# Scratch places given out by a planner's clock instead of a count of instructions, with the planner's durations booked anew

## The chip, the cores and the metric

The kernel runs on one core of one Trainium2 chip. The metric is device time in microseconds (us) from the first to the last instruction of one execution, with what lies around it; the time before is the median of three runs. Shorter is better.

## The reference, cut to what matters

One inference step of a one-layer hybrid decoder, all in float32, for a prompt of 272 positions (16 learned meta tokens and 256 tokens) and for 8 sequences of 4 new tokens: 304 columns in all, each 2048 long.

```
xn = rms_norm(x, norm_mix);  z = xn @ w_in             # 2048 -> 7456 columns
z_a, z_b = z[..., :RWKV_COLS], z[..., RWKV_COLS:]
o_a, S_a = rwkv7_mixer(z_a, shifted z_a, S_a0, ...)    # 16 heads of 64, a recurrence over positions
o_b, S_b = retention_mixer(z_b, S_b0, ...)             # 4 heads of 256, in chunks
h = x + concat([o_a, o_b]) @ w_out
hn = rms_norm(h, norm_ffn)
h = h + (silu(hn @ w_gate) * (hn @ w_up)) @ w_down     # 2048 -> 5632 -> 2048
y = rms_norm(h, norm_final)                            # and the new states
```

The weights are read once, 512 KB at a time. They and the activations are split into a high and a low part (`hi` and `lo`, of a type that TensorE takes in one pass), so a weight tile of 128 by 128 costs three matmuls: high by high, high by low, low by high.

## The kernel before

**Two kinds of work.** `main` (L609) walks through the weights in a fixed sequence: the input projection (59 column tiles), the output projection, then gate, up and down of the feed-forward part. For each step it loads (`wr`, four buffers), casts on ScalarE (`wh`), subtracts on VectorE (`wl`, the two with four buffers each) and issues three matmuls into an accumulator `acc`. Beside it run *streams*: Python generators that do the mixing of the finished columns. There is one for each of 8 pairs of RWKV heads (`pair` with `inverse`, `units`, `sample`, `pair_out`), one for each of 4 retention heads (`ret`), and small ones that empty an accumulator (`evacuate`, `mixed`) or bring a pair's small weights (`lora_weights`). Their matmuls go to `mm`. All streams belong to the first part of the run, in which TensorE has the input projection to do between them.

**What sets the order.** The kernel builds itself twice. In a first pass, the draft, a `Plan` books every instruction on a clock of its own for each engine: `book` (L346) works out when the operands are ready and adds a duration from a small table; `array` does so for TensorE. `pick` (L422) is asked before every step of `main`: the first stream whose booked time of readiness has passed goes on to its next `yield`, else `main` takes a step. The choices go into a log, and the second pass, which writes the real program, replays it. Every engine then runs its own instructions strictly in that order, and an instruction that waits holds up all behind it on its engine. Loads and stores are all issued by SyncE (SP), also in order.

**Where scratch lives.** Tiles of the streams come from `Step.t` (L550). In the draft each gets a tensor of its own. `Room.place` (L470) then gives each a place in one of two long tiles, the arenas (`arena_dt.float` for F32 and `arena_dt.float32r` for F32R in the profile, 33000 columns together), so that tiles whose lives don't overlap may share columns. A life here runs from the tile's creation (`note`) to its last use (`use`), both counted in instructions booked so far by all engines, plus a slack of 40, 20, 10, 5 or 0 instructions, whichever first fits; among five orders of packing the smallest is taken. The count says which instruction comes first in the program. It doesn't say which comes first in time, since engines run apart by microseconds. So the layer that writes the program must make the first writer of a place wait, with semaphores, until the last reader of the tile that had it before is done. The draft doesn't know these waits, since its tiles share nothing.

Helpers record every instruction, so that all have one line in the profile (L300); tiles tell them apart. Names used below: `lora` is the DRAM tensor of the pairs' small weights (two loads for each pair, by `lora_weights`), `s0w` the RWKV states (one for each pair), `s0r` the retention states (four for each retention head) and `rmask` its masks (one for each head). In `inverse`, five `stream_shuffle` instructions fill a tile `rs` three times for each pair, GpSimd multiplies from it, and VectorE then writes the masked tiles `em`.

Of the kernel before, what the change touches and what calls it, by code (L numbers as in the profile page):

```python
# [9 lines left out]
F32R = mybir.dt.float32r  # L10
# [65 lines left out]
KEYS = ((0, META, SEQ, 0), (P, P, NP - P, SEQ), (LASTK, 2 * P, T - 2 * P, SEQ + NP - P))  # L76
RMW = SEQ + NP - P + T - 2 * P
ROOM = 33000


def zcols():
# [53 lines left out]
def constants():  # L135
# [169 lines left out]
class Plan:  # L305
# [5 lines left out]
    def __init__(self, nc, rooms, draft, log, keep):  # L311
        self.keep = keep
        self.rooms, self.draft, self.log, self.count = rooms, draft, log, 0
        self.clock = dict(PE=0.0, DVE=0.0, ACT=0.0, POOL=0.0, SP=0.0)
        self.end = self.dma = 0.0
        self.uses, self.outside = {}, ()
# [29 lines left out]
    def book(self, eng, what, a, k):  # L346
        self.count += 1
        if not self.draft:
            return
        aps = [x for x in (*a, *k.values()) if hasattr(x, "shape")]  # L350
        for x in aps:
            for room in self.rooms.values():
                room.use(x, self.count)
        out, ins = aps[0], aps[1:]

        at = 0.0
        boxes = [(x.name, self.box(x), x is out) for x in aps if x.name not in self.outside]
        meet = lambda a, b: a[0] < b[1] and b[0] < a[1] and a[2] < b[3] and b[2] < a[3]
        for name, box, writes in boxes:
            for other, done, by, written in self.uses.get(name, ()):  # L360
                if (written or writes) and done + 100 > at and not (by == eng == "PE") and meet(box, other):
                    at = max(at, done + (30 if by == eng else 100 if eng == "PE" else 60))
        n = math.prod(out.shape[1:])
        if eng == "PE":
            done = self.array(what, *a[:3], at) + 170
        elif eng == "SP":
            self.clock[eng] = at = max(self.clock[eng] + 400, at)
            self.dma = max(self.dma, at + 1400) + 4 * out.shape[0] * n / 320
            done = self.dma + 600
# [84 lines left out]
class Room:  # L454

    def __init__(self):
        self.spans, self.index, self.places, self.size, self.taken = [], {}, None, 0, 0

    def note(self, ap, size, count):
        self.index[ap.name] = len(self.spans)
        self.spans.append([size, count, count])

    def use(self, x, count):
        i = self.index.get(getattr(x, "name", None))
        if i is not None:
            self.spans[i][2] = count

    def place(self, limit):  # L470


        for slack in (40, 20, 10, 5, 0):
            best = None
            for key in (lambda n, a, b: (-n, a), lambda n, a, b: (-n * (b - a), a), lambda n, a, b: (a - b, -n),
                        lambda n, a, b: (a, -n), lambda n, a, b: (-n // 256, a - b)):
                size, places = self.pack(key, slack)
                if best is None or size < best[0]:
                    best = size, places
            if best[0] <= limit:  # L480
                break
        self.size, self.places = best
        assert self.size <= limit, self.size

    def pack(self, key, slack):
        done, places = [], [0] * len(self.spans)
        for i in sorted(range(len(self.spans)), key=lambda i: key(*self.spans[i])):
            size, a, b = self.spans[i]
            size = -(-size // 8) * 8
# [6 lines left out]
            places[i] = at  # L496
            done.append((at, size, a, b))
        return max(o + n for o, n, _, _ in done), places

    def take(self, size):  # L500

# [14 lines left out]
class Step:  # L516
# [33 lines left out]
    def t(self, shape, tag, dt=F32, bufs=None, pool=None):  # L550
        self.n += 1
        if pool is not None:
            name = f"{tag}_{self.n}"
            old = self.tags.setdefault(tag, [])
            old.append(name)
            n = {"mm": 8 - ACC, "acc": ACC}.get(tag, bufs)
            if n and len(old) > n:
                self.plan.follows(name, old[-1 - n])
            return pool.tile(shape, dt, tag=tag, name=name, **({} if bufs is None else {"bufs": bufs}))
        size = math.prod(shape[1:])  # L560
        if self.draft:
            ap = self.mp.tile(shape, dt, tag=f"t{self.n}", name=f"{tag}_{self.n}")
            self.rooms[dt].note(ap, size, self.plan.count)
# [1148 lines left out]
def body(tc, I, O):  # L1712
    from contextlib import ExitStack
    gam4 = constants()[3]
    rooms = {F32: Room(), F32R: Room()}
    nc = draft(I, O)
    log = []
    Step(tile.TileContext(nc[0]).__enter__(), nc[1], nc[2], ExitStack(), rooms, True, log).build(gam4)
    rooms[F32R].place(4200)
# [25 lines left out]
```

## Time and profile before

| what | us |
|---|---|
| median of 3 runs (lowest, highest) | 1593.91 (1592.52, 1594.58) |
| the profiled execution's own time | 1595.29 |
| its span, first to last instruction | 1593.5 |
| TensorE (PE) busy | 1547.0, 97% |
| VectorE (DVE) busy | 1101.9, 69% |
| ScalarE (ACT) busy | 822.2, 52% |
| GpSimd (POOL) busy | 166.5, 10% |
| DMA, mean over the span | 158 GB/s, 252.49 MB |

The granted clock of TensorE is 0.996 of full speed over the run. Up to about 600 us the input projection and all mixing run side by side; after that only the output projection and the feed-forward part are left, and GpSimd has no work there. An entry `x <- y` in a list of waits is idle time of engine x that ended when y was done, and a bracket at the end of a row of the timeline gives the idle time just before that row. "issue" means that nothing was waited for that the profile shows.

### The profile page before, as it was taken

To read this page: it belongs to the slowest core of one execution; us is meant where nothing else is said; L and a number is where in the kernel's file an instruction comes from. 1 tells how busy PE (TensorE), PEld (TensorE's weight loads), DVE (VectorE), ACT (ScalarE), POOL (GpSimd) and SP (SyncE) were. 2 spreads that over 40 slices of the span, in tenths; PEclk is the share of its full clock that TensorE was granted. 3 is DMA by queue.
4 is the path that set the end of the run, shared out by engine and by line. 5 is a ranking of instruction groups with operands and counts; after the bars stand their busy time and mean duration, and the time that the engine had idled before them with its cause. 6 is when DMAs were issued, how large, how long until landed. Compare 5 with 4: busy or idle time off the path is not lost.

```text
span 1593.5 us, 30795 instructions
## 1 busy us (share of the span) xinstructions
PE 1547.0 (97%) x11388; PEld 1506.5 (95%) x11388; DVE 1101.9 (69%) x2590; ACT 822.2 (52%) x1795; POOL 166.5 (10%) x567
## 2 busy tenths in 40 slices
PE   9999999999999999999999999999999999999997
PEld 8888999898888899999999999999999999999997
DVE  7888888897879867777565656565655656565657
ACT  6657676747656564455444444444444444444445
POOL 0343414323041300000000000000000000000000
PEclk9999999999999999999999999999999999999998
DMA  7443343334543448655555555555555555555553
GB/s 263 144 123 112 114 126 113 101 113 133 157 156 117 143 149 278 231 163 157 169 164 165 168 170 159 169 166 168 166 166 172 160 165 167 172 162 170 162 168 116
DMA packets 76998, 252.49 MB, mean 158 GB/s; under 512 B 9392, under 2 KB 14640, under 8 KB 76848
## 3 DMA queue, kind: packets, MB, share of 16 engines
q1 hardware_dynamic: 76848, 250.52, 50.8%
q8 instruction: 90, 1.47, 0.4%
q14 instruction: 60, 0.49, 0.1%
HBM read 236.21 MB, written 14.28 MB: 157 GB/s over the span
## 4 chain that ended last, share of the span: by engine, by line
PE 71%; DVE 6%; DMA 2%; ACT 1%; issue 1%; POOL 1%; DVEq 0%; POOLq 0%; ACTq 0%; SPq 0%
PE acc L300 66%; PE mm L300 5%; DVE arena_dt.float L300 5%; DVE wl L300 1%; ACT arena_dt.float L300 1%; DMA arena_dt.float<-s0r 1%; POOL arena_dt.float L300 1%; DMA arena_dt.float<-lora 1%; DVE arena_dt.float32r L300 0%; ACT wh L300 0%; DVE xl L300 0%; ACT arena_dt.float32r L300 0%; DVEq L1741 0%; POOL shout L300 0%; POOLq L300 0%
## 5 line engine op out<-in xcount | busy, mean ns | idle before, releaser
L300 PE MATMUL acc<-xh,wh 128*128 128x288 f32 (+2 forms) x2592 | 791.7, 305 | 0.6 <-ACT wh L300 0.6
L300 PE MATMUL acc<-xh,wl 128*128 128x288 f32 (+2 forms) x2592 | 772.8, 298 | 13.3 <-DVE wl L300 13.2
L300 PE MATMUL acc<-xl,wh 128*128 128x288 f32 (+2 forms) x2592 | 766.8, 296 | 0.0
L300 ACT CAST wh<-wr 128x512 fp32r<-128x512 f32 x826 | 500.9, 617 | 363.8 <-PE acc L300 327.7
L300 DVE TENSOR_TENSOR wl<-wr,wh 128x512 fp32r<-128x512 f32 x826 | 562.8, 689 | 127.8 <-ACT wh L300 124.8
L300 PEld LDWEIGHTS acc<-xh,wl 128*128 128x128 f32 x2592 | 486.1, 188 | 19.7 <-DVE wl L300 18.9
L300 PEld LDWEIGHTS acc<-xh,wh 128*128 128x128 f32 x2592 | 487.8, 188 | 5.9 <-issue 1.3
L300 PEld LDWEIGHTS acc<-xl,wh 128*128 128x128 f32 x2592 | 486.9, 188 | 3.7 <-issue 0.5
L300 PE MATMUL acc<-arena_dt.float32r,wh 128*128 128x288 f32 x1408 | 280.0, 294 | 0.4 <-ACT arena_dt.float32r L300 0.3
L300 PEld LDWEIGHTS acc<-arena_dt.float32r,wh 128*128 128x128 f32 x1408 | 226.3, 188 | 0.9 <-ACT arena_dt.float32r L300 0.6
L300 PE MATMUL acc<-arena_dt.float32r,wl 128*128 128x288 f32 x704 | 208.0, 295 | 0.0
L300 DVE TENSOR_TENSOR arena_dt.float<-acc,arena_dt.float 128x288 f32<-128x288 f32 (+4 forms) x181 | 72.8, 420 | 167.1 <-PE acc L300 166.2
L300 PE MATMUL mm<-arena_dt.float 128*128 128x128 f32 (+6 forms) x1072 | 172.0, 311 | 15.4 <-ACT arena_dt.float L300 5.9
L300 PEld LDWEIGHTS mm<-arena_dt.float 128*128 128x128 f32 (+1 forms) x1072 | 138.1, 181 | 32.7 <-ACT arena_dt.float L300 8.5
L300 DVE TENSOR_TENSOR arena_dt.float<-arena_dt.float 128x288 f32<-128x288 f32 (+10 forms) x483 | 158.5, 355 | 10.8 <-ACT arena_dt.float L300 4.3
L300 DVE TENSOR_TENSOR arena_dt.float<-arena_dt.float,acc 128x288 f32<-128x288 f32 x208 | 94.4, 454 | 100.4 <-PE acc L300 99.9
L300 ACT ACTIVATE arena_dt.float<-arena_dt.float 128x288 f32<-128x288 f32 (+6 forms) x200 | 85.2, 433 | 122.7 <-DVE arena_dt.float L300 115.5
L300 ACT COPY arena_dt.float<-mm 64x64 f32<-64x64 f32 (+11 forms) x330 | 91.7, 286 | 80.6 <-PE mm L300 74.9
L300 PEld LDWEIGHTS acc<-arena_dt.float32r,wl 128*128 128x128 f32 x704 | 132.4, 188 | 0.0
L300 ACT CAST arena_dt.float32r<-arena_dt.float 128x288 fp32r<-128x288 f32 (+4 forms) x73 | 30.4, 423 | 124.2 <-DVE arena_dt.float L300 92.6
L300 POOL TENSOR_TENSOR arena_dt.float<-arena_dt.float 128x75 f32<-128x75 f32 (+14 forms) x240 | 86.9, 362 | 73.1 <-DVE arena_dt.float L300 50.1
L300 POOL MEMSET arena_dt.float<- 128x64 f32 (+8 forms) x137 | 29.7, 238 | 181.3 <-DVE arena_dt.float L300 102.9
(64 smaller groups left out, 675.5 us busy)
## 6 DMA issues: line engine op xcount, KB each, us to landing
wr<-big SPq DMA_DIRECT2D x409, 512.0 KB, 3.6
arena_dt.float<-s0r SPq DMA_DIRECT2D x16, 512.0 KB, 5.1
out_rts<-arena_dt.float SPq DMA_DIRECT2D x16, 512.0 KB, 5.6
arena_dt.float<-xT SPq DMA_DIRECT2D x4, 576.0 KB, 5.8
out_y<-arena_dt.float SPq DMA_DIRECT2D x8, 288.0 KB, 2.2
arena_dt.float<-xT SPq DMA_DIRECT2D x7, 304.0 KB, 6.2
wr<-big SPq DMA_DIRECT2D x8, 256.0 KB, 5.7
arena_dt.float<-lora SPq DMA_DIRECT2D x16, 128.0 KB, 3.5
```

Of the source, the lines that this page charges most:

```text
L300: return self._plan.keep(f(*a, **k))
```

## The change

**Time instead of count.** `use` is handed, besides the count, the booked start and end of the instruction (`self.begun` for TensorE, else the engine's clock less 400 ns; `done`), and a tile's life begins at its first use rather than at its creation; a tile never used gets no place. `pack` still forbids overlap in the program's order. But two tiles that follow each other in a place are now also compared by the clock: `free` is the booked time between the last use of the one and the first use of the other. A place with `free` of at least `gap` is taken at once, from below; if there is none, the place with the most `free`. `place` tries five orders of packing (one of the keys is new) with gaps of 2000, 1000, 500, 200 and 0 ns, and keeps the packing with the least `lack`, which is the sum over all tiles of what is missing to 800 ns. The size of the arenas is bounded as before.

**Durations.** `book` prices some instructions anew: VectorE's `tensor_scalar` from scratch at 0.56 instead of 1.05 ns an element; 67 ns (VectorE) or 90 ns (ScalarE) more for an operand with one element per partition; 40 ns less for ScalarE where it reads PSUM; GpSimd's copies and arithmetic less; 80 instead of 110 ns more for instructions on fewer than 128 partitions. `banks` holds the names of PSUM tiles for this. The rest of the draft, `pick`, `main` and all streams stay as they are; but since `pick` reads the clock, the log comes out another way.

```diff
@@ book
-        for x in aps:
-            for room in self.rooms.values():
-                room.use(x, self.count)
...
+            each = sum(math.prod(x.shape[1:]) == 1 for x in ins) if n > 1 else 0
             if eng == "DVE":
                 big = max(math.prod(x.shape[1:]) for x in aps)
+                per = 0.56 if what == "tensor_scalar" and ins[0].name not in self.banks else 1.05
...
-                             "tensor_tensor_scan": (65 + 2.1 * n, 85)}.get(what, (62 + 1.05 * n, 83))
+                             "tensor_tensor_scan": (65 + 2.1 * n, 85)}.get(what, (62 + per * n + 67 * each, 83))
             elif eng == "ACT":
-                dur, tail = 108 + 0.83 * n, 94
+                dur, tail = 108 + 0.83 * n + 90 * each - 40 * (ins[0].name in self.banks), 94
             else:
-                dur, tail = (60 + 0.85 * n, 60) if what == "memset" else (260 + 2.4 * n, 60)
+                dur, tail = (60 + 0.85 * n, 60) if what == "memset" else (185 + 0.8 * n, 60) if what == "tensor_copy" else (265 + 2 * n, 60)
             if part and eng != "POOL":
-                dur += 110
+                dur += 80
...
+        for x in aps:
+            for room in self.rooms.values():
+                room.use(x, self.count, self.begun if eng == "PE" else self.clock[eng] - 400, done)
@@ Room
-    def use(self, x, count):
+    def use(self, x, count, at, done):
...
+        span = self.spans[i]
+        if span[1] is None:
+            span[1], span[3] = count, at
+        span[2], span[4] = count, max(span[4], done)
@@ pack
-            b += slack
-            at = 0
-            for o, n, c, d in sorted(x for x in done if x[2] <= b and a <= x[3]):
-                if o - at >= size:
-                    break
-                at = max(at, o + n)
+            for o, n, c, d, s, u in done:
+                if a <= d and c <= b:
+                    near.append((o, o + n, -1.0))
+                else:
+                    free = max(0.0, at - u if d < a else s - until)
+                    if free < gap:
+                        near.append((o, o + n, free))
...
+                free = min((f for s, e, f in near if s < o + size and o < e), default=gap)
+                if free > -1.0 and (best is None or free > best[0]):
+                    best = free, o
+                    if free >= gap:
+                        break
...
+            lack += max(0.0, FREE - best[0])
```

No instruction is added or taken away: each engine has as many as before. What moves is their order, and what they wait for. Two places show it.

SP's queue where the first retention head's loads stand, with the semaphores that each row waits for (`DVE`, `PE`, `Pool` and `Activation` are engines, `DMAHW` earlier transfers). Before:

```order
L300 DMA wr_4899<-big 128x1024 [waits DMAHW3_49,DVE_49]
L300 DMA arena_dt.float_70<-lora 128x256 [waits DMAHW2_49,PE_49]
L300 DMA arena_dt.float_70<-s0w 128x512
L300 DMA arena_dt.float_70<-s0r 128x1024 [waits DMAHW2_49,DMAHW4_49,DVE_49,Pool_49]
L300 DMA arena_dt.float_70<-s0r 128x1024 [waits DMAHW5_49]
L300 DMA arena_dt.float_70<-s0r 128x1024 [waits DMAHW6_49,DVE_49,PE_49]
L300 DMA arena_dt.float_70<-s0r 128x1024 [waits DMAHW7_49,DVE_49,Pool_49]
L300 DMA wr_5118<-big 128x1024 [waits DMAHW0_49]
```

The same place now:

```order
L302 DMA wr_4868<-big 128x1024 [waits DMAHW1_49,DVE_49]
L302 DMA arena_dt.float_70<-s0r 128x1024
L302 DMA arena_dt.float_70<-s0r 128x1024 [waits DMAHW2_49]
L302 DMA arena_dt.float_70<-s0r 128x1024 [waits DMAHW3_49]
L302 DMA arena_dt.float_70<-s0r 128x1024 [waits DMAHW4_49]
L302 DMA arena_dt.float_70<-lora 128x256 [waits DMAHW5_49,DVE_49,PE_49]
L302 DMA arena_dt.float_70<-s0w 128x512 [waits DMAHW7_49,DMAHW6_49,DVE_49]
L302 DMA out_rws<-arena_dt.float_70 128x512
L302 DMA wr_4992<-big 128x1024 [waits DMAHW0_49,Activation_49]
```

The four loads of `s0r` stand ahead of `lora` and `s0w`, and none of them waits for an engine any more, where three did. `lora` and `s0w` still wait for engines. Over the whole queue, 31 of the 44 scratch loads (16 `lora`, 8 `s0w`, 16 `s0r`, 4 `rmask`) waited for an engine before, and 17 do now; 14 of them waited for VectorE, now 4; 18 for GpSimd, now 9; 15 for TensorE, now 15.

VectorE's queue in `inverse` of a late pair, where the two `em` tiles (rows with `cst`, 128x256) are written after the recurrence of another pair (the two rows of 64x64). Before:

```order
L300 SCALAR_TENSOR_TENSOR arena_dt.float_70<-mm_6787,arena_dt.float_70 64x64 [waits PE_49]
L300 SCALAR_TENSOR_TENSOR arena_dt.float_70<-mm_6787,arena_dt.float_70 64x64
L300 TENSOR_TENSOR arena_dt.float_70<-arena_dt.float_70,cst_262 128x256 [waits Pool_49]
L300 TENSOR_TENSOR arena_dt.float_70<-arena_dt.float_70,cst_262 128x256
L300 TENSOR_TENSOR arena_dt.float_70<-acc_6682,arena_dt.float_70 128x304 [waits DMAHW3_49,PE_49]
L300 TENSOR_TENSOR arena_dt.float_70<-acc_6682,arena_dt.float_70 128x304
L300 TENSOR_TENSOR arena_dt.float_70<-arena_dt.float_70 128x32 [waits DVE_49]
L300 TENSOR_TENSOR wl_6814<-wr_6620,wh_6813 128x512 [waits Activation_49]
```

Now:

```order
L302 SCALAR_TENSOR_TENSOR arena_dt.float_70<-mm_6724,arena_dt.float_70 64x64 [waits PE_49]
L302 SCALAR_TENSOR_TENSOR arena_dt.float_70<-mm_6724,arena_dt.float_70 64x64
L302 TENSOR_TENSOR wl_6729<-wr_6492,wh_6728 128x512 [waits Activation_49]
L302 TENSOR_TENSOR arena_dt.float_70<-arena_dt.float_70,cst_262 128x256 [waits DVE_49]
L302 TENSOR_TENSOR arena_dt.float_70<-arena_dt.float_70,cst_262 128x256
L302 SCALAR_TENSOR_TENSOR arena_dt.float_70<-arena_dt.float_70 128x288
L302 TENSOR_TENSOR wl_6762<-wr_6535,wh_6761 128x512 [waits DMAHW7_49,Activation_49]
```

The first `em` waited for GpSimd and now waits only for VectorE itself, and a `wl` subtraction of the weights stands in front of it. Elsewhere on this queue, the rows of `stream_shuffle` that wait for GpSimd, 8 before, are 1 now.

More of the change, by code (lines that the diff above doesn't have):

```diff
@@ L78 @@
 ROOM = 33000
+WIDE = 4200
+FREE, GAPS = 800.0, (2000.0, 1000.0, 500.0, 200.0, 0.0)
 def zcols():
@@ L315, in __init__ @@
         self.end = self.dma = 0.0
-        self.uses, self.outside = {}, ()
+        self.uses, self.outside, self.banks = {}, (), set()
         self.mode, self.parts, self.empty, self.begun, self.idle = None, {}, 0.0, 0.0, 0.0
@@ L459, in __init__, with note @@
         self.spans, self.index, self.places, self.size, self.taken = [], {}, None, 0, 0
-    def note(self, ap, size, count):
+    def note(self, ap, size):
         self.index[ap.name] = len(self.spans)
-        self.spans.append([size, count, count])
-    def use(self, x, count):
+        self.spans.append([size, None, 0, 0.0, 0.0])
+    def use(self, x, count, at, done):
         i = self.index.get(getattr(x, "name", None))
-        if i is not None:
-            self.spans[i][2] = count
-    def place(self, limit):
-        for slack in (40, 20, 10, 5, 0):
-            best = None
[L475 to L480, printed above, removed]
-                break
-        self.size, self.places = best
-        assert self.size <= limit, self.size
@@ L485, in pack @@
[L485 to L489, printed above, removed]
-            b += slack
-            at = 0
-            for o, n, c, d in sorted(x for x in done if x[2] <= b and a <= x[3]):
-                if o - at >= size:
-                    break
-                at = max(at, o + n)
-            places[i] = at
-            done.append((at, size, a, b))
-        return max(o + n for o, n, _, _ in done), places
+        if i is None:
+            return
@@ new lines, in use @@
+        span = self.spans[i]
+        if span[1] is None:
+            span[1], span[3] = count, at
+        span[2], span[4] = count, max(span[4], done)
+    def place(self, limit):
+        best = None
+        for key in (lambda n, a, b, *_: (-n, a), lambda n, a, b, *_: (-n * (b - a), a), lambda n, a, *_: (a, -n),
+                    lambda n, a, b, *_: (a - b, -n), lambda n, a, b, *_: (-n // 256, a - b)):
+            for gap in GAPS:
+                found = self.pack(key, limit, gap)
+                if found is not None and (best is None or found[0] < best[0]):
+                    best = found
+        self.lack, self.size, self.places = best
@@ new lines, in pack @@
+    def pack(self, key, limit, gap):
+        done, places, lack, end = [], [0] * len(self.spans), 0.0, 0
+        used = [i for i, span in enumerate(self.spans) if span[1] is not None]
+        for i in sorted(used, key=lambda i: key(*self.spans[i])):
+            size, a, b, at, until = self.spans[i]
+            size = -(-size // 8) * 8
+            near = []
+            for o, n, c, d, s, u in done:
[5 more added lines that the diff above has]
+                        near.append((o, o + n, free))
+            near.sort()
+            best = None
+            for o in sorted({0, *(e for _, e, _ in near)}):
+                if o + size > limit:
+                    break
+                free = min((f for s, e, f in near if s < o + size and o < e), default=gap)
[3 more added lines that the diff above has]
+                        break
+            if best is None:
+                return None
+            lack += max(0.0, FREE - best[0])
+            places[i] = best[1]
+            end = max(end, best[1] + size)
+            done.append((best[1], size, a, b, at, until))
+        return lack, end, places
@@ L553, in t @@
             name = f"{tag}_{self.n}"
+            if tag in ("mm", "acc"):
+                self.plan.banks.add(name)
             old = self.tags.setdefault(tag, [])
@@ L562, in t @@
             ap = self.mp.tile(shape, dt, tag=f"t{self.n}", name=f"{tag}_{self.n}")
-            self.rooms[dt].note(ap, size, self.plan.count)
+            self.rooms[dt].note(ap, size)
             return ap
@@ L1718, in body @@
     Step(tile.TileContext(nc[0]).__enter__(), nc[1], nc[2], ExitStack(), rooms, True, log).build(gam4)
-    rooms[F32R].place(4200)
+    rooms[F32R].place(WIDE)
     rooms[F32].place(ROOM - rooms[F32R].size)
```

## The prediction

> **What bounds the kernel now.** I read the page first, then busy time by stretches, then the list of waits of TensorE and, for its longest ones, the timeline backwards.
>
> ```profile
> span 1593.5 us, 30795 instructions
> ```
>
> ```profile
> 0.00:40.00 40.00, 37.45 (x251) 34.71 (x252) 29.63 (x59) 25.10 (x45) 2.07 (x9) 1.00 0.77 262
> 40.00:320.00 280.00, 263.26 (x1858) 249.16 (x1856) 235.88 (x741) 186.91 (x493) 104.91 (x344) 1.00 0.40 118
> 320.00:600.00 280.00, 265.70 (x1887) 245.90 (x1888) 227.12 (x663) 172.61 (x464) 59.53 (x216) 0.99 0.44 140
> 600.00:1540.00 940.00, 938.38 (x7082) 935.47 (x7081) 572.54 (x1054) 410.49 (x737) 0.00 (x0) 1.00 0.57 173
> 1540.00:1593.50 53.50, 42.24 (x317) 41.28 (x316) 36.76 (x77) 27.09 (x56) 0.00 (x0) 0.90 0.38 126
> ```
>
> The columns are the stretch, its length, then busy time of TensorE, its weight loads, VectorE, ScalarE and GpSimd, granted clock, DMA share and GB/s. TensorE is the bound. From 600 to 1540 us it is idle for 940 - 938.38 = 1.6 us: nothing to gain. The opening lacks 2.6 us and the ending 11.3 us; the change has no lever there, since nearly all scratch is used before 600 us. In the mixing stage, 40 to 600 us, TensorE lacks 560 - 263.26 - 265.70 = 31.0 us. That is all that better places can win. VectorE is busy there for 463.0 of 560 us, 83%, so it has little air and any wait on it soon reaches TensorE.
>
> TensorE's waits in that stage (engine and line, what it waited for, us, times, longest):
>
> ```profile
> PE acc L300 <- DVE wl L300: 12.1, 19, 1.2
> PE mm L300 <- ACT arena_dt.float L300: 6.8, 8, 1.7
> PE mm L300 <- POOL arena_dt.float L300: 4.6, 4, 1.6
> PE mm L300 <- DVE arena_dt.float L300: 2.0, 4, 1.2
> PE mm L300 <- DMA arena_dt.float<-s0r: 1.9, 4, 0.9
> ```
>
> These name the last link only. Whether places are behind them has to be followed back. The eleven rows of the timeline with over 1 us of idle time in front:
>
> ```profile
> 95.33 0.41 PE L300 MATMUL acc<-xh,wl 128*128 128x304 f32 x1 [1.18 <-DVE wl L300]
> 113.46 0.74 PE L300 MATMUL mm<-arena_dt.float 128*128 128x64 f32 x5 [1.05 <-POOL arena_dt.float L300]
> 199.63 0.49 PE L300 MATMUL mm<-arena_dt.float 128*128 128x128 f32 x2 [1.72 <-ACT arena_dt.float L300]
> 232.75 0.49 PE L300 MATMUL mm<-arena_dt.float 128*128 128x128 f32 x2 [1.06 <-ACT arena_dt.float L300]
> 282.59 0.63 PE L300 MATMUL mm<-arena_dt.float 128*128 128x64 f32 x4 [1.26 <-issue]
> 298.39 0.89 PE L300 MATMUL mm<-arena_dt.float 128*128 128x256 f32 x3 [1.58 <-POOL arena_dt.float L300]
> 406.38 0.48 PE L300 MATMUL mm<-arena_dt.float,cst 128*128 128x288 f32 x1 [1.26 <-POOL arena_dt.float L300]
> 424.03 0.49 PE L300 MATMUL mm<-arena_dt.float 128*128 128x128 f32 x2 [1.53 <-ACT arena_dt.float L300]
> 497.71 0.40 PE L300 MATMUL acc<-xh,wl 128*128 128x288 f32 x1 [1.17 <-DVE wl L300]
> 535.05 0.41 PE L300 MATMUL acc<-xh,wl 128*128 128x304 f32 x1 [1.08 <-DVE wl L300]
> 538.84 0.35 PE L300 MATMUL mm<-arena_dt.float 128*128 128x128 f32 x1 [1.18 <-DVE arena_dt.float L300]
> ```
>
> Together 14.07 us. Two of them followed back. First 406.38:
>
> ```profile
> 402.96 0.52 DVE L300 TENSOR_TENSOR arena_dt.float<-arena_dt.float 128x256 f32<-128x256 f32 x2
> 403.07 0.33 SPq L300 DMA_DIRECT2D arena_dt.float<-lora  x1
> 405.19 0.40 ACT L300 CAST arena_dt.float32r<-arena_dt.float 128x256 fp32r<-128x256 f32 x1 [2.71 <-DMA arena_dt.float<-lora]
> 405.62 0.43 DVE L300 TENSOR_TENSOR arena_dt.float32r<-arena_dt.float,arena_dt.float32r 128x256 fp32r<-128x256 f32 x1 [2.14 <-ACT arena_dt.float32r L300]
> 406.11 0.21 POOL L300 MEMSET arena_dt.float<- 128x128 f32 x1 [3.86 <-DVE arena_dt.float32r L300]
> ```
>
> A load from DRAM reads no scratch; if it waits for an engine, it waits for its place. By the table of places that `pack` makes, this `lora` load got columns that VectorE's mixing of another pair was still reading, and was issued just behind it, at 403.07. ScalarE stood 2.71 us for the data, VectorE 2.14 us behind ScalarE, GpSimd 3.86 us, TensorE 1.26 us. A memset reads nothing either: GpSimd's wait too is one for a place. Then 535.05 and 538.84:
>
> ```profile
> 528.54 4.61 POOL L300 TENSOR_TENSOR arena_dt.float<-arena_dt.float 128x35 f32<-128x35 f32 x13
> ...
> 532.66 0.76 DVE L300 TENSOR_TENSOR arena_dt.float<-arena_dt.float,cst 128x256 f32<-128x256 f32 x2 [2.71 <-POOL arena_dt.float L300]
> ...
> 534.30 0.69 DVE L300 TENSOR_TENSOR wl<-wr,wh 128x512 fp32r<-128x512 f32 x1
> ```
>
> `em` (532.66) is made from `mt` and a constant; neither comes from GpSimd. It waits 2.71 us because its place held what GpSimd's multiplications were still working on. The `wl` behind it in VectorE's order is late, and TensorE stands 1.08 and then 1.18 us.
>
> **The change part by part.** *Places.* Done the same way for all eleven with the table of places: behind seven (113.46, 232.75, 298.39, 406.38, 424.03, 535.05, 538.84; 8.74 us) stands a place wait as long as the wait itself or longer; behind 95.33, 199.63 and 282.59 a shorter one, 1.2 us together; behind 497.71 none. That is 9.94 of 14.07 us, 71%. I take the same share for the shorter waits: 0.71 x 31.0 = 22.0 us of TensorE's idle time rest on places.
>
> How much of that goes? Three groups show what kind of waits are meant:
>
> ```profile
> ACT arena_dt.float32r L300 <- DMA arena_dt.float<-lora: 29.7, 10, 5.2
> ```
>
> ```profile
> DVE arena_dt.float L300 <- POOL arena_dt.float L300: 10.5, 10, 3.4
> ```
>
> ```profile
> L300 POOL MEMSET arena_dt.float<- 128x128 f32 (+8 forms) x136 | 29.6, 239 | 152.4 <-DVE arena_dt.float L300 74.1 <-PE mm L300 69.7 <-DVE arena_dt.float32r L300 6.4
> ```
>
> By the orders shown above, scratch loads that wait for an engine fall from 31 to 17, those that wait for VectorE from 14 to 4; shuffles that wait for GpSimd from 8 to 1. So a half to nearly all go, by kind; GpSimd's 152.4 us matter least, since GpSimd is idle most of the time anyway. And where a place wait goes, the next condition is late by less, but not by nothing: without the wait for its place, the `lora` load still takes about 2 us to land (403.07 to 405.19). Between a half and nearly all I take 60%, nearer to the half because of what is next: 0.6 x 22.0 = 13 us. Ends: 15% (3 us), if what is next is nearly as late; 100% and 4 us of the other waits, 26 us.
>
> Tiles that live from their first use shorten lives; that gives the packer room and costs no time on the chip. The arenas stay in their bound, and no instruction is added.
>
> *Durations.* The new prices change the draft's clock, hence the order in which streams advance. Rows to judge them by (mean ns of one):
>
> ```profile
> L300 DVE TENSOR_SCALAR arena_dt.float<-arena_dt.float 128x288 int32<-128x288 int32 (+4 forms) x54 | 17.4, 325 | 1.0
> ```
>
> ```profile
> L300 ACT COPY arena_dt.float<-mm 64x64 f32<-64x64 f32 (+11 forms) x330 | 91.7, 286 | 80.6 <-PE mm L300 74.9
> ```
>
> A `tensor_scalar` of 288 was booked at 62 + 302 + 83 = 447 ns, now at 62 + 161 + 83 = 306; the trace has 325. That is closer. A 64-element copy from PSUM was booked at 255, now at 215; the group's mean, over wider forms too, is 286, so this one may now be too short. The steps move by a few tenths of a us each; I cost this at nothing, between 2 us of gain (54 x 0.14 = 7.6 us of misbooking set right, a quarter of it felt) and the loss in the slower rival below. The cover is the weights made ahead: `wl` is cast up to three tiles ahead of TensorE; if that cover is gone, each tenth of a us late on VectorE is a tenth on TensorE.
>
> *A rule against it.* GpSimd's work no longer waits as long and falls beside other VectorE work than before. `wl` reads two operands from scratch and is VectorE's largest group; in the mixing stage, and from 700 to 1500 us where GpSimd has no work:
>
> ```profile
> L300 DVE TENSOR_TENSOR wl<-wr,wh 128x512 fp32r<-128x512 f32 x205 | 141.3, 692 | 31.4 <-ACT wh L300 30.7
> ```
>
> ```profile
> L300 DVE TENSOR_TENSOR wl<-wr,wh 128x512 fp32r<-128x512 f32 x503 | 342.0, 688 | 82.5 <-ACT wh L300 80.6
> ```
>
> GpSimd at its side costs 4 ns x 205 = 0.8 us in all, and that is in the time already; a shift of it can cost no more. The Trainium skill, "SBUF — State Buffer", section "Who interferes with whom", says that a VectorE instruction with two inputs in SBUF and a GpSimd instruction that reads SBUF exclude each other for the whole instruction. By that rule freed GpSimd work would stop `wl` for whole instructions; the two rows don't show it.
>
> *The sum.* 1595.3 (the profiled execution) - 13 = 1582.3 us. The median of the runs lies 1.4 us below that execution, so 1581 us.
>
> **The rivals.**
>
> *Larger gain (0.10).* TensorE has more room than its busy time shows: by the rows above, weight loads are busy 249.16 + 245.90 = 495.1 of 560 us, 64.9 us short against 31.0. If matmuls draw together once nothing holds them, the gain is 0.6 x 0.71 x 64.9 = 28 us: 1566 us. Against it: from 600 to 1540 both counts are full, while in the mixing stage float32 matmuls stand between, in which weight loads have gaps with nobody waiting. The Trainium skill, "Perfetto Trace Analysis", section "Identifying the Most-Contended Engine", says to judge TensorE by the busy share of weight loads, not of matmuls; this is what that rule would make of the stage.
>
> *No change (0.07).* The place waits lie behind others as late: TensorE's waits keep their sum and get other names. About 1594 us (1591 to 1597). For it: of the waits followed back, 497.71 has no place behind it, and VectorE at 83% has queues of its own. Against it: seven of eleven.
>
> *Slower (0.09).* The streams run ahead of the engines. If copies from PSUM are booked 0.07 us short (286 - 215), 330 of them bring later steps forward by 23 us in sum; engines in order then wait at their heads, ScalarE for TensorE's `mm` first, and half of that, 11.6 us, reaches TensorE. With only 3 us from places: 1595.3 + 11.6 - 3 - 1.4 = 1602.5 us. It decides against the change once more than 13 us come back this way. For it: the group of copies already has 80.6 us of idle time in front, 74.9 for `mm`. Against it: 286 is a mean over wider forms, and most prices move towards the trace.
>
> That the change doesn't do what it says is ruled out by the rows of the orders: the waits are gone from them.
>
> **How the numbers follow.** The forecast has 0.74. A measurement of this kernel can tell about 0.2% from no change (3.2 us; its three runs spread over 2.1). The forecast's own range goes from 1569 (26 us gained) to 1591 (3 us). The range for 8 in 10 leaves out most of the larger gain, below, and slower, above, and takes in part of no change: 1569 to 1592. Faster by over 0.2% (below 1590.7) are the forecast, the larger gain and nothing else: 0.84. Within 0.2%: 0.07. Slower: 0.09.
>
> **What would show it.** Right: TensorE's idle time from 40 to 600 us falls from 31.0 to about 18; ScalarE's 29.7 us for `lora` fall to 10 to 15; VectorE's 10.5 us for GpSimd to below 4; the stage ends about 13 us earlier and everything after 600 us keeps its length. Wrong: the list of TensorE's waits keeps its sum with other names (no change), or ScalarE's and VectorE's waits for `mm` grow by over 13 us (slower), or TensorE's busy time in the stage itself shrinks (larger gain).

## The result and the profile after

| | before | after |
|---|---|---|
| median of the runs | 1594.24 us (1592.52 to 1595.34, 4 runs) | 1576.96 us (1574.73 to 1579.24, 4 runs) |
| ratio, 95% interval | | 0.9893 [0.9875, 0.991] |
| profiled execution / its span | 1595.29 / 1593.5 us | 1577.13 / 1575.2 us |

The change makes the kernel faster by 17.3 us; 13 were forecast, to 1581 us. First the page's span and TensorE's busy time, then the same five stretches as before (columns as in the prediction):

```profile
span 1575.2 us, 30747 instructions
...
PE 1542.0 (98%) x11388; PEld 1506.9 (96%) x11388; DVE 1101.2 (70%) x2590; ACT 821.8 (52%) x1795; POOL 177.4 (11%) x567
```

```profile
0.00:40.00 40.00, 37.47 (x251) 34.96 (x252) 29.66 (x60) 25.35 (x46) 2.54 (x14) 1.00 0.74 263
40.00:320.00 280.00, 269.63 (x1907) 257.35 (x1906) 242.38 (x760) 189.64 (x503) 114.36 (x351) 0.99 0.40 122
320.00:600.00 280.00, 275.05 (x2000) 259.25 (x1998) 239.84 (x687) 179.47 (x475) 60.51 (x203) 1.00 0.48 154
600.00:1540.00 940.00, 935.77 (x7053) 931.73 (x7052) 563.98 (x1031) 409.47 (x734) 0.00 (x0) 1.00 0.56 171
1540.00:1575.20 35.20, 24.05 (x187) 23.64 (x185) 25.37 (x57) 17.84 (x38) 0.00 (x0) 0.87 0.32 116
```

In the mixing stage TensorE now lacks 560 - 269.63 - 275.05 = 15.3 us, 15.7 less than the 31.0 of before. From 600 to 1540 us it lacks 4.2 us instead of 1.6. TensorE's busy time over the whole span is 1542.0 us, where the page of before has 1547.0. (The page counts 48 instructions less than that of before. They are waits for semaphores; each engine has as many of its own as before.) So of the 18.3 us that the span lost, 13.3 are idle time of TensorE and 5.0 are busy time. TensorE's waits from 40 to 600 us:

```profile
PE acc L302 <- DVE wl L302: 7.5, 15, 1.1
PE mm L302 <- ACT arena_dt.float L302: 4.0, 3, 2.5
PE mm L302 <- DVE arena_dt.float L302: 1.2, 2, 0.8
```

The waits on GpSimd's scratch (4.6 us) and on `s0r` (1.9 us) are gone from the list, and the one for `wl` is down from 12.1 to 7.5. Of the eleven waits over 1 us three are left, and one of 0.93 us that has a place behind it still (VectorE stands 2.16 us at 373.19 until a store of states, `out_rws`, is done with the columns):

```profile
193.70 0.79 PE L302 MATMUL mm<-arena_dt.float 128*128 128x128 f32 x2 [2.50 <-ACT arena_dt.float L302]
...
259.37 0.40 PE L302 MATMUL acc<-xh,wl 128*128 128x288 f32 x1 [1.06 <-DVE wl L302]
...
301.25 0.40 PE L302 MATMUL acc<-xh,wh 128*128 128x288 f32 x1 [1.01 <-ACT wh L302]
...
375.77 1.13 PE L302 MATMUL mm<-arena_dt.float 128*128 128x128 f32 x8 [0.93 <-ACT arena_dt.float L302]
```

VectorE has no wait on GpSimd's scratch left (10.5 us before). ScalarE's wait for `lora`, then GpSimd's memsets and VectorE's `wl` in the stage:

```profile
ACT arena_dt.float32r L302 <- DMA arena_dt.float<-lora: 19.9, 9, 5.8
```

```profile
L302 DVE TENSOR_TENSOR wl<-wr,wh 128x512 fp32r<-128x512 f32 x219 | 151.4, 692 | 33.6 <-ACT wh L302 33.3
L302 POOL MEMSET arena_dt.float<- 128x128 f32 (+8 forms) x135 | 28.8, 240 | 25.1 <-PE mm L302 14.9 <-DVE arena_dt.float32r L302 4.1 <-DMA out_rws<-arena_dt.float 3.8
```

GpSimd stood 152.4 us ahead of its memsets before and stands 25.1 now. A good part of that has only moved: ahead of its copies to `shout` it stands 102.3 us, where it stood 51.1. A `wl` takes 692 ns as before.

What is new lies behind 600 us. TensorE's rows there, then SP's queue of DMA issues ahead of them:

```profile
611.70 0.63 PE L302 MATMUL mm<-arena_dt.float 128*32 128x256 f32 x4 [2.04 <-DMA arena_dt.float<-s0r]
612.94 1.46 PE L302 MATMUL mm<-arena_dt.float 128*32 128x256 f32 x12 [0.62 <-DMA arena_dt.float<-s0r]
```

```profile
597.34 1.51 SPq L302 DMA_DIRECT2D arena_dt.float<-s0r  x2
599.30 0.38 SPq L302 DMA_DIRECT2D arena_dt.float<-xT  x1
600.84 0.33 SPq L302 DMA_DIRECT2D wr<-big  x1
601.83 1.84 SPq L302 DMA_DIRECT2D arena_dt.float<-s0r  x2
```

The last head's four loads of `s0r` are two and two now, with a load of `xT` and one of the weights (`wr`) between; TensorE waits 2.66 us for the second two.

### The profile page after: what moved, and what is told of

It reads as the page before. It is cut to its first block, busy times and chain, and to the rows that moved or that the text cites. A ratio compares the mean times of both kernels' runs of the same rounds, so it can differ in the third digit from the quotient of the medians.

```text
span 1575.2 us, 30747 instructions
## 1 busy us (share of the span) xinstructions
PE 1542.0 (98%) x11388; PEld 1506.9 (96%) x11388; DVE 1101.2 (70%) x2590; ACT 821.8 (52%) x1795; POOL 177.4 (11%) x567
## 4 chain that ended last, share of the span: by engine, by line
PE 82%; DVE 11%; ACT 3%; DMA 2%; issue 2%; SPq 0%; POOL 0%; DVEq 0%; ACTq 0%; POOLq 0%
PE acc L302 73%; PE mm L302 9%; DVE arena_dt.float L302 8%; DVE wl L302 3%; ACT arena_dt.float L302 2%; DMA arena_dt.float<-xT 1%; DMA arena_dt.float<-lora 1%; DMA arena_dt.float<-s0r 1%; ACT wh L302 1%; SPq L302 0%; DMA out_rwp<-arena_dt.float 0%; DVE xl L302 0%; POOL arena_dt.float L302 0%; DVE arena_dt.float32r L302 0%; ACT arena_dt.float32r L302 0%
## 5 line engine op out<-in xcount | busy, mean ns | idle before, releaser
L302 PE MATMUL mm<-arena_dt.float 128*128 128x128 f32 (+6 forms) x1072 | 168.5, 311 | 8.7 <-ACT arena_dt.float L302 3.4
L302 DVE TENSOR_TENSOR arena_dt.float<-arena_dt.float 128x288 f32<-128x288 f32 (+12 forms) x483 | 159.9, 355 | 9.7 <-ACT arena_dt.float L302 4.5
L302 ACT COPY arena_dt.float<-mm 64x64 f32<-64x64 f32 (+7 forms) x330 | 91.9, 287 | 80.7 <-PE mm L302 76.8
L302 POOL TENSOR_TENSOR arena_dt.float<-arena_dt.float 128x75 f32<-128x75 f32 (+14 forms) x240 | 91.7, 382 | 97.1 <-DVE arena_dt.float L302 57.3
L302 POOL COPY arena_dt.float<-arena_dt.float 128x32 f32<-128x32 f32 (+5 forms) x123 | 36.5, 328 | 109.8 <-DVE arena_dt.float L302 75.1
```

The costliest lines, as they stand in the source:

```text
L302: return self._plan.keep(f(*a, **k))
```

## The experiments

Two theories. *Places*: the gain comes from the time between two uses of a place; the new durations, and tiles that live from first use, are worth nothing. *Order*: the durations change the order of the streams, and that carries part of the gain or costs part of it. Ratios are against the kernel before on the same chip. "Idle" is TensorE's idle time in the profiled execution.

| kernel | order from | places by | median us | ratio, 95% interval | idle 40-600 | idle 600-1540 |
|---|---|---|---|---|---|---|
| before | old durations | count, slack 0 | 1594.24 | 1 | 31.0 | 1.6 |
| after | new | clock, 2000 ns | 1576.96 | 0.9893 [0.9875, 0.991] | 15.3 | 4.2 |
| e1_places | old | clock | 1570.77 | 0.9852 [0.9837, 0.9868] | 13.3 | 1.5 |
| e7_seeds | old | clock, more packings | 1569.71 | 0.984 [0.9827, 0.9853] | 9.8 | 1.5 |
| e9_count | old | count, slack 10 | 1577.10 | 0.9891 [0.987, 0.9912] | 17.9 | 1.5 |
| e2_durations | new | count, slack 20 | 1583.28 | 0.9929 [0.9916, 0.9942] | 17.7 | 4.4 |
| e6_slack0 | new | count, slack 0 | 1612.47 | 1.0114 [1.01, 1.0128] | 38.6 | 3.7 |
| e4_nogap | new | clock, gap 0 | 1618.96 | 1.0157 [1.014, 1.0174] | 39.2 | 4.7 |
| e3_created | new | clock, lives from creation | 1575.05 | 0.9883 [0.9866, 0.9899] | 15.8 | 4.0 |
| e5_dma | new, DMA booked longer | clock | 1578.12 | 0.9901 [0.9887, 0.9915] | 18.7 | 1.6 |
| e8_states | new, `s0r` moved | clock | 1572.58 | 0.9863 [0.9848, 0.9878] | 15.6 | 1.8 |

In the traces e1, e7 and e9 have the instructions of every engine in the order of before, and e2, e3, e4, e6 and e8 in that of after; e5 has an order of its own. Each kernel stands for one packing.

**Places alone (e1_places).** The old durations with the new places. At the old order none of the five packing orders fits with any gap, so two shuffled ones stand beside them:

```diff
-                dur, tail = 108 + 0.83 * n + 90 * each - 40 * (ins[0].name in self.banks), 94
+                dur, tail = 108 + 0.83 * n, 94
...
-                    lambda n, a, b, *_: (a - b, -n), lambda n, a, b, *_: (-n // 256, a - b)):
+                    lambda n, a, b, *_: (a - b, -n), lambda n, a, b, *_: (-n // 256, a - b), mixed(1), mixed(36)):
```

(and the other duration lines likewise; `mixed` is `-(n ** p) * ((b - a + 1) ** q)` times a random factor from 0.5 to 1.5).

> The order of before (old durations), with places given out by the clock. At the old durations none of the five orders of packing fits with any time between, so one more order, by area with a seeded shuffle, is added; it fits with 2000 ns. If the place waits carry the gain, most of it is here: 1577 to 1583 us, and TensorE's idle time from 40 to 600 us is 15 to 20 us. If the new order carries it, 1591 to 1596 us and about 30 us idle.

1570.77 us, below both ranges: the places alone give 24 us, more than the whole change. The instructions stand in the order of before, so only the places, and the waits that come with them, can have done it. Two stretches, and TensorE's longest waits from 40 to 600 us:

```profile
40.00:600.00 560.00, 546.71 (x3920) 517.96 (x3919) 482.95 (x1450) 370.39 (x982) 175.69 (x556) 1.00 0.45 141
600.00:1540.00 940.00, 938.47 (x7084) 935.52 (x7083) 568.16 (x1039) 413.13 (x743) 0.00 (x0) 1.00 0.55 170
```

```profile
PE mm L303 <- ACT arena_dt.float L303: 5.3, 4, 2.0
PE acc L303 <- DVE wl L303: 4.1, 12, 0.7
```

Idle time is 13.3 and 1.5 us: the 4.2 us that after has behind 600 us come from the new order.

**Durations alone (e2_durations).** The old `Room` and its `use`, with the new duration lines.

```diff
-                room.use(x, self.count, self.begun if eng == "PE" else self.clock[eng] - 400, done)
+                room.use(x, self.count)
...
+        for slack in (40, 20, 10, 5, 0):
```

> The order of the changed kernel (new durations), with places given out by the count of instructions, as before. If the place waits carry the gain: 1590 to 1598 us, 28 to 33 us idle on TensorE from 40 to 600 us, and VectorE waits again for GpSimd by about 10 us. If the order carries it: 1575 to 1581 us.

1583.28 us, between the two ranges: a miss for both, and places as the whole cause had left no room for it. But with the new order the old rule packs with a slack of 20 instructions, where before found room for 0. So it had time between uses by another way, and said nothing against places yet. That needed e6.

**The new order without slack (e6_slack0).** As e2, but

```diff
-        for slack in (40, 20, 10, 5, 0):
+        for slack in (0,):
```

> The durations-only kernel with its slack forced to 0 instructions. The kernel before packs only at slack 0 (28144 of 28952 columns; at 5 it needs 29048); with the new durations a slack of 20 fits (28624), so durations alone brought time between uses in by the back door. If that is what its gain of 11.5 us was made of, the gain goes: 1592 to 1606 us, TensorE idle over 28 us from 40 to 600 us. If the new order itself is better, it stays at 1580 to 1586 us.

1612.47 us, above the range and 18 above before. The order is that of e2, so the gain of e2 was the slack. Whether the new order is the worse one where places are tight is not shown: this packing is tighter as well (27240 columns by its planner, before 28144). Its stretch, and VectorE's wait that was 10.5 us before and none after:

```profile
40.00:600.00 560.00, 521.45 (x3648) 488.15 (x3649) 451.77 (x1371) 352.57 (x944) 162.84 (x554) 0.98 0.41 127
```

```profile
DVE arena_dt.float L300 <- POOL arena_dt.float L300: 11.0, 22, 1.4
```

**No time asked (e4_nogap).** After, taking the lowest free place:

```diff
-FREE, GAPS = 800.0, (2000.0, 1000.0, 500.0, 200.0, 0.0)
+FREE, GAPS = 800.0, (0.0,)
```

> The changed kernel with no time asked for between two uses: lives from first use and the new durations stay, each tile takes the lowest free place. If time between the uses is what counts: 1594 to 1606 us, as slow as before or slower, since the slack of 40 instructions is gone too. If lives from first use or the order count: 1576 to 1582 us.

1618.96 us, above the range too, and 42 above after by one number. It packs tightest (27168 columns, before 28144, of 28952) and is the slowest of all. TensorE's longest waits from 40 to 600 us:

```profile
PE mm L302 <- ACT arena_dt.float L302: 17.4, 10, 3.1
PE acc L302 <- DVE wl L302: 10.7, 20, 1.2
PE mm L302 <- DVE arena_dt.float L302: 3.6, 4, 2.3
```

Beside after's 4.0, 7.5 and 1.2: the old last links are back, ScalarE's scratch first.

**Lives from creation (e3_created).** `note` keeps the count at which a tile is made, and that is its start:

```diff
-            span[1], span[3] = count, at
+            span[1], span[3] = self.made[i], at
```

> The changed kernel with lives in the program's order from the tile's creation again; places by the clock and new durations stay. The lack goes from 7.2 to 7.7 booked us only. If lives from first use are no more than room for the packer: 1574 to 1580 us, no difference. If they are a part of the gain: 1581 us or more.

1575.05 us, its runs (1573.73 to 1579.65) across those of after: lives from first use made no difference that these runs can tell.

**Longer transfers (e5_dma).** To move the `lora` and `s0r` loads' places by what they wait for:

```diff
-            self.dma = max(self.dma, at + 1400) + 4 * out.shape[0] * n / 320
+            self.dma = max(self.dma, at + 2200) + 4 * out.shape[0] * n / 260
```

> The changed kernel with transfers booked as traced: 2200 instead of 1400 ns ahead, 260 instead of 320 bytes per ns. ScalarE still waits 19.9 us for lora loads in the mixing stage of the changed kernel, and TensorE 2.7 us for s0r just behind it. If streams that step on before their load has landed are what is left, those fall below 10 us and the time is 1572 to 1575 us. If those waits lie off the path, or the new order undoes it: 1575 to 1580 us.

A miss: 1578.12 us, no gain. ScalarE's wait for `lora` went up and not down:

```profile
ACT arena_dt.float32r L302 <- DMA arena_dt.float<-lora: 26.7, 14, 4.9
```

The booking also moved the order: TensorE's idle time rose from 15.3 to 18.7 us in the stage and fell from 4.2 to 1.6 behind it. So this run prices neither the transfers nor the wait. That little hangs on the wait shows elsewhere: ScalarE waits 24.4 us for `lora` in e1 and 24.3 in e7, and these two are the fastest.

**The last head's `s0r` (e8_states).** After, with the second two loads issued directly behind the first two, for that head only:

```diff
         states()
+        if h == RH - 1:
+            states()
...
-        states()
+        if h < RH - 1:
+            states()
```

> The changed kernel with all four loads of retention states of the last head issued together, so that no load of weights stands between them in the queue of SyncE; nothing else moves there. In the changed kernel two stand behind such a load at 600.84 us and TensorE then waits 2.04 and 0.62 us for them near 611 us. If that is the new order's loss against the old one, 2 to 3 us of it come back: 1574 to 1575 us. If it is hidden anyway: 1576 to 1578 us.

1572.58 us, below the range and 4.4 below after. SP's queue has the four together, and TensorE's wait is 0.21 us:

```profile
596.93 2.76 SPq L302 DMA_DIRECT2D arena_dt.float<-s0r  x4
```

```profile
608.89 1.06 PE L302 MATMUL mm<-arena_dt.float 128*32 128x256 f32 x12 [0.21 <-DMA arena_dt.float<-s0r]
```

Idle time there fell by 4.2 - 1.8 = 2.4 us only; the last section shows what the rest is.

**More packing orders (e7_seeds).** As e1, with sixty shuffled orders, and gaps of 2000 or 1000 ns only:

```diff
-                    lambda n, a, b, *_: (a - b, -n), lambda n, a, b, *_: (-n // 256, a - b), mixed(1), mixed(36)):
+                    lambda n, a, b, *_: (a - b, -n), lambda n, a, b, *_: (-n // 256, a - b), *map(mixed, range(60))):
...
-            for gap in GAPS:
+            for gap in GAPS[:2]:
```

> Places by the clock at the old durations as in the first experiment, with 60 shuffled orders of packing instead of 2: the lack falls from 9.1 to 5.4 booked us. If what is left of place waits still costs, 1566 to 1570 us; if the best packing is past the point where places matter, 1569 to 1573 us, no difference from 1570.8.

1569.71 us, the best version here and below both kernels. The two ranges overlap and it lies in both, and its interval overlaps that of e1: whether the better packing gained anything over e1, these runs can't tell.

```profile
40.00:600.00 560.00, 550.17 (x3944) 520.69 (x3943) 483.76 (x1452) 372.44 (x985) 175.79 (x555) 1.00 0.46 144
```

Idle time in the stage is 9.8 us, 21.2 less than before.

**Does it need the clock? (e9_count).** Before, order, durations and rule by count, with the sixty shuffled packing orders, so that a slack of 10 instructions fits:

```diff
-        for slack in (40, 20, 10, 5, 0):
+        for slack in (10, 5, 0):
...
-                        lambda n, a, b: (a, -n), lambda n, a, b: (-n // 256, a - b)):
+                        lambda n, a, b: (a, -n), lambda n, a, b: (-n // 256, a - b), *map(mixed, range(60))):
```

> The order and the durations of before, with places by the count of instructions as before, but 60 shuffled orders of packing more, so that a slack of 10 instructions fits where before only 0 did. No clock is read. If any distance between two uses does it, most of the gain of the places-only kernel (24 us) is here: 1573 to 1582 us. If it takes the clock, because instructions counted near each other run far apart in time: 1586 to 1595 us.

1577.10 us: a distance of ten instructions gives 17 of the 24 us, and the clock the other 6 (e1). GpSimd's memsets from 40 to 600 us:

```profile
L301 POOL MEMSET arena_dt.float<- 128x1 f32 (+8 forms) x135 | 29.3, 238 | 125.9 <-PE mm L301 55.5 <-DVE arena_dt.float L301 42.2 <-DMA out_rts<-arena_dt.float 17.9
```

GpSimd still stands 125.9 us for its places (152.4 before), and the time fell by 17 us all the same. In e1 most of that wait is gone, too, and GpSimd stands ahead of its copies instead:

```profile
L303 POOL COPY arena_dt.float<-arena_dt.float 128x32 f32<-128x32 f32 (+4 forms) x119 | 37.0, 342 | 130.6 <-DVE arena_dt.float L303 74.6 <-DMA out_rws<-arena_dt.float 38.8 <-DMA out_rtp<-arena_dt.float 8.3
L303 POOL MEMSET arena_dt.float<- 128x1 f32 (+8 forms) x135 | 29.0, 241 | 23.7 <-DVE arena_dt.float L303 21.8
```

Ahead of memsets, of these copies and of those to `shout` it stands 125.9 + 58.2 + 53.8 = 237.9 us in e9 and 23.7 + 130.6 + 107.0 = 261.3 us in e1, which is the faster by 6 us. So most of these waits lie off the path. Of the 44 scratch loads, 31 still name an engine in what they wait for, as many as before.

## Why the prediction was right, and where its terms were off

- **TensorE's idle time in the mixing stage rests on places: right.** The prediction put 22.0 of 31.0 us on them; the best packing at the old order took 21.2 (e7).
- **"Between a half and nearly all I take 60%": too little.** After took 15.7 of the 22.0 us (71%), e1 17.7 and e7 21.2. That "what is next is nearly as late", its lower end, did not hold: where a place wait went, most of the wait went.
- **The durations, "I cost this at nothing": this term failed.** With the clock's places the new order costs 1576.96 - 1570.77 = 6.2 us by the medians (e1 has the two packing orders more). In the profiled executions, without what the granted clock took (last section), after stands at 1573.7 us, e8 at 1571.1 and e1 at 1569.5: 4.2 us, of which 2.6 are the last head's second two loads of `s0r`, behind a weight load in SP's queue. The prediction named the cover of the weights, and not the order of loads in that queue. What the other 1.6 us are was not tried. "Everything after 600 us keeps its length" fell by the same loads.
- **The sum had idle time only.** TensorE's busy time fell by 5.0 us as well, which no term held. The granted clock doesn't explain it (last section: after lost more to it than before). e1 shows where it goes, since its matmuls are those of before one by one. They are busy for 6.5 us less. Those that had idle time in front of them in before and have none in e1 make 6.8 us of that, all others together -0.3; TensorE stands idle 65 times in before and 39 times in e1. A first matmul behind a wait is busy for 0.40 us in the rows above, where matmuls in a row start 0.13 apart (last section). So each wait that goes takes about a quarter of a us of busy time with it, as far as the profile's modelled ends of matmuls can be trusted. That the 5.0 us of after are the same wasn't followed matmul by matmul.
- **Why 13 came near 17.3:** too little for places (13 for 24 by e1) and nothing for the order (6.2 lost) work against each other, and the 5.0 us of busy time came on top. The mechanism was right and the lever was the one named; that the total came so near is luck in part.
- **The three signs.** Idle time of about 18 us: 15.3. VectorE's wait for GpSimd below 4: none. ScalarE's wait for `lora` of 10 to 15: 19.9, a miss, though the two fastest kernels wait longer for it (24.4 and 24.3). The count of loads that wait for an engine, 31 to 17, had been taken as the size of the effect by kind; e9 gains 17 us with 31. A semaphore that an instruction names is not time that it waits.
- **The rivals.** No change is ruled out by the interval. For slower, "waits for `mm`" should have grown by over 13 us: ScalarE's is 67.2 where it was 68.9, VectorE's 18.9 where it was 24.3:

```profile
ACT arena_dt.float L302 <- PE mm L302: 67.2, 64, 4.0
...
DVE arena_dt.float L302 <- PE mm L302: 18.9, 18, 3.0
```

  But the order's loss is this rival's kind, with another mechanism: a load late in a queue. Its price also rested on a misreading: a 64x64 copy is on 64 partitions, for which `book` adds 110 ns, now 80, so it was booked at 365 and is now at 295, not 255 and 215. This form alone takes 205, so it is still booked long and not short:

```profile
L300 ACT COPY arena_dt.float<-mm 64x64 f32<-64x64 f32 x112 | 23.0, 205 | 11.9 <-PE mm L300 9.4 <-POOL arena_dt.float L300 0.7
```

  The larger gain was there for better packings (24 us in e1). Its sign, a shrinking busy time, came too, but at 5.0 us in after and 6.5 in e1, where the rival had 64.9 - 31.0 = 33.9 us of room: most of the gain is TensorE's idle time. The forecast's own lower end is 1568 by its sum (1595.3 - 26 - 1.4), not 1569.
- **The rule against it**, that VectorE and GpSimd exclude each other, was rightly left out of the sum: in the stage a `wl` takes 692 ns in both kernels, while GpSimd's busy time rose from 164.4 to 114.36 + 60.51 = 174.9 us. But "can cost no more" than 0.8 us was too strong, since 4 ns is a mean over all. The 64 `wl` of before that have GpSimd's arithmetic or copies beside them for over 300 ns take 705 ns, the 132 with none 687; after has 78 of the first kind, at 705.
- **First use** cost nothing and gave nothing (e3).

## What to carry to other kernels

When scratch is shared by in-order engines, the distance between two uses of a place is part of the schedule: at the same order the tightest packing was slower by 42 us than one that asks for time (e4, after), and even ten instructions of distance gave most of the gain (e9), so spend the free columns on it. Judge such waits at the bounding engine: GpSimd stood 238 us ahead of the same three groups in e9 and 261 in the faster e1. A planner's costs and its places are two changes: test them apart, and look at what a new order does to loads that share a queue.

## What the runs showed of the hardware

A short wait of TensorE can cost more than its length. In the kernel before, two stretches of 4 us around the wait at 406.38 (the third number is TensorE's busy time, the last but two the granted clock), and TensorE's rows behind it:

```profile
404.00:408.00 4.00, 2.19 (x12) 1.44 (x11) 2.38 (x5) 2.73 (x7) 0.21 (x1) 1.00 0.11 33
408.00:412.00 4.00, 4.00 (x17) 3.67 (x16) 2.84 (x8) 1.18 (x4) 0.00 (x0) 0.57 0.67 170
420.00:424.00 4.00, 2.50 (x20) 2.27 (x18) 3.51 (x8) 1.66 (x5) 0.00 (x0) 1.00 0.46 93
424.00:428.00 4.00, 3.90 (x28) 3.71 (x28) 3.27 (x8) 3.37 (x8) 0.00 (x0) 1.00 1.02 389
```

```profile
404.68 0.30 PE L300 MATMUL acc<-xl,wh 128*128 128x304 f32 x1
404.81 0.30 PE L300 MATMUL acc<-xh,wl 128*128 128x304 f32 x1
...
408.97 0.46 PE L300 MATMUL acc<-xl,wh 128*128 128x304 f32 x1
409.22 0.46 PE L300 MATMUL acc<-xh,wl 128*128 128x304 f32 x1
```

After 1.81 us of idle time within 4, the granted clock is 0.57 over the next 4 us: (1 - 0.57) x 4 = 1.7 us lost, and matmuls that started 0.13 us apart start 0.25 apart. After 1.50 us, from 420 on, nothing is lost.

What decides is where the idle time falls. In after's trace the clock is at a half from 193.63 and from 613.47 us, for 3.413 us each time; the two lie 419.84 us apart, 123.0 times 3.413. In every trace all such losses lie on a grid of this step, which has another start in each execution. The steps of after around its waits at 193.70 and 611.70:

```profile
190.22:193.63 3.41, 0.99 (x8) 0.75 (x6) 1.93 (x6) 1.84 (x6) 1.05 (x3) 1.00 0.77 245
193.63:197.04 3.41, 3.34 (x14) 3.34 (x15) 2.46 (x8) 1.74 (x5) 0.00 (x0) 0.50 0.21 87
610.06:613.47 3.41, 1.15 (x14) 0.49 (x16) 0.15 (x1) 0.00 (x0) 0.00 (x0) 1.00 0.84 342
613.47:616.88 3.41, 3.41 (x18) 2.60 (x13) 0.80 (x2) 2.20 (x5) 0.00 (x0) 0.50 0.03 8
```

The steps of e3, which has the same order and the same waits (2.80 us up to 193.29, then 1.82 and 0.62 us up to 610.91):

```profile
188.60:192.01 3.41, 1.89 (x15) 1.66 (x13) 2.37 (x9) 0.68 (x3) 1.89 (x10) 1.00 0.90 269
192.01:195.42 3.41, 2.13 (x16) 2.13 (x17) 2.52 (x7) 2.58 (x7) 0.00 (x0) 1.00 0.39 138
608.49:611.90 3.41, 1.61 (x17) 0.54 (x17) 0.00 (x0) 0.00 (x0) 0.00 (x0) 1.00 0.71 292
```

In after each wait falls into one step, with 2.42 and 2.26 us idle, and the next step runs at a half: 0.5 x 3.41 = 1.7 us lost, twice. In e3 a step ends inside the first wait, which leaves 1.52 and 1.28 us on its two sides, and the step of the second has 1.80; nothing is lost. Some losses in e4, e5 and e6 last two steps. Over the eleven traces, from 8 to 1530 us, no step with less than 1.7 us of idle time brought on a loss, every one with over 1.95 did, and between the two some did.

So what a wait costs depends on the execution. After's profiled execution took 1577.13 us with two losses, that of e3 1573.73 with none: 3.4 us, the two losses. That of e8, 1571.08, has none either and lies 2.6 below e3, about the 2.4 us of idle time that it took away. The rest of the 4.4 us between the medians of e8 and after is then of the clock's size, though the other executions have no trace to show it. From 40 to 600 us before, after, e1 and e2 lost 1.7 us each, e5 and e9 3.4, e4 and e6 8.5, and e3, e7 and e8 nothing; from 600 to 1540 only after, e2 and e4 lost anything, 1.7 us each.

The Trainium skill, "TensorE: Matmul & The Clock Gate", section "HAM oscillation — how this bites in real kernels", gives as the rule no idle gap of TensorE over about 3.4 us. The loss of half of some 3.4 us agrees with its window; the gap does not: here 1.26 and 0.55 us close together were enough.
